# Two transfers within HBM behind each attention product: a GpSimd copy as the gate

## The chip, the cores and the metric

The kernel runs on one core of one Trainium2 chip. The metric is device time in microseconds from the first to the last instruction of the core, with what lies around them. Three runs of the kernel before took 528.51, 530.26 and 531.51 us (median 530.26 us). About 0.5% of that, 2.65 us, is what a comparison of two such kernels can tell from no change.

## The reference, cut to what matters

One decoder layer over 512 tokens of width 1024. The input is normalized, and one large projection gives the inputs of two mixers that run side by side. Mixer A is sparse attention with 8 heads in 2 groups of 4 (a compressed, a selected and a sliding branch), mixer B is retention with 4 heads in chunks of 128 tokens. Each is gated, projected and merged through a sigmoid gate per channel.

```python
h = rms_norm(x, norm_pre)
proj = h @ w_in
(q_n, k_c, v_c, k_s, v_s, k_w, v_w, g_n, z_n,
 q_r, k_r, v_r, z_r, m_a, m_b) = jnp.split(proj, split_points(), axis=-1)
...
y_a = (o_a * jax.nn.silu(z_n)) @ w_nsa_o
...
y_b = (o_b * jax.nn.silu(z_r)) @ w_ret_o
merged = jax.nn.sigmoid(m_a) * y_a + jax.nn.sigmoid(m_b) * y_b
x = x + rms_norm(merged @ w_out, norm_post)
```

The product `o_a * silu(z_n)` is formed here in eight pieces, one for each tile of 128 tokens and each group of heads. Two halves of the projections that give `m_a` and `m_b` (the blocks MA1 and MB1) are computed with seven products of sub-blocks in place of eight; for that, sums and differences of blocks of `w_in` are needed.

## The kernel before, in words

All large operands are float32, split into a high part (float32r) and a low part; a product is three matmuls (high by high, low by high, high by low). Weights come in as a stream of 512 KB tiles `raw` (four buffers) that SyncE's queue loads from HBM (line 354). A tile is cast in two halves to `whi` (mostly by ScalarE, line 197), VectorE subtracts to get `wlo` (line 209, called by `sub_split`), and a buffer comes free for the next load when both `wlo` are made.

**The order of instructions** is worked out while the kernel is built. A class `Order` holds coroutines with priorities (`od.spawn`), keeps an estimated time for TensorE (`now`), for each other engine and for the transfers, and at each step lets the first coroutine go on whose awaited time has come. What a coroutine yields is a time to wait for, a time with an engine (`yield e, "pool"` waits as well until that engine is estimated to be less than 0.7 us behind), or a condition. `od.op("pool", 900.0)` adds to GpSimd's estimate. These estimates fix only the order in which instructions stand on each engine. At run time an engine starts its next instruction when the one ahead is through and its semaphores are there.

**The stages** on TensorE: projections of the attention inputs, `hidden` (compression of keys and values), then blocks of projections (Z, MA, ZR, QK, VR ...) into which the attention heads are woven (`att_head`, `att_block`), then retention (`ret`) woven into the next blocks, then the output blocks and the final product.

**The attention product.** `att_sum` runs once for each token tile t = 3, 2, 1, 0 and group g = 0, 1. When the last product of that piece is in its PSUM bank (`bank_93` for one, `bank_94` for the next), ScalarE copies one half, VectorE adds the other (`nat<-bank,nat`, 64x512) and VectorE multiplies by the gate in place (`arena_l<-nat,arena_l`, 64x512). When all eight are there, retention may read its scores.

**The sums of weights.** `weight_sums` makes, for two blocks, the sums in HBM: eight steps, at each of them one transfer for each block, 16 in all, each of 512 KB within HBM, issued by GpSimd. Steps 0 to 3 are copies (line 334), steps 4 to 7 add to what is there (line 336; steps 6 and 7 read sums made earlier). The results (`t`) are loaded by SyncE into `raw` from 383 us on, in `seven`. The planned times are `T0 + TSTEP * k` = 110, 122, ... 290 us, in the planner's own time; nothing but the order on GpSimd's queue and the earlier step on the same data holds a transfer back at run time.

**GpSimd's other work** in that stretch is the power -0.5 of the group norm of retention, `rv<-rv,nhalf` (line 209, two columns): `ret` takes mean and variance on VectorE, GpSimd makes `rv`, and VectorE's next instructions scale the retention output by it (`arena_l<-bank,mv,rv`, line 218); the gated result is transposed on TensorE (`bank<-ident,arena_l`, line 234).

Of the kernel before, what the change touches and what calls it, by code (L numbers as in the profile page):

```python
# [10 lines left out]
FT = mybir.dt.float32  # L11
# [7 lines left out]
P = 128  # L19
# [18 lines left out]
SLACK = 700.0  # L38
WAKE = 7
HOLD = 1500.0  # L40
T0, TSTEP = 110000.0, 12000.0
DVE_BIAS = 400


# [95 lines left out]
def block_kernel(ctx: ExitStack, tc, x, xT, x0s, ws, small, w2s, norm_post, rope_r, dmask, out):  # L140
    nc = tc.nc
    V, S, G, T, DMA = nc.vector, nc.scalar, nc.gpsimd, nc.tensor, nc.sync

    sp = ctx.enter_context(tc.tile_pool(name="small", bufs=1))
# [15 lines left out]
    def at(kb, n, dt=FT):  # L160
        o = int(kb * 256)
        if dt == FR:
            return arena_r[:, o:o + n]
        assert o >= 28 * 256 or o + n <= 28 * 256
        return arena_f[:, o - 28 * 256:o - 28 * 256 + n] if o >= 28 * 256 else arena_l[:, o:o + n]
# [6 lines left out]
    od = Order()  # L172
# [23 lines left out]
    def act(o, i, func=AF.Copy, r=0.0, **kw):  # L196
        S.activation(o, i, func, **kw)  # L197
        return od.op("act", act_ns(o, i, lazy(kw.get("bias"), kw.get("scale"))) + (95 if "accum_out" in kw else 0), r)
# [9 lines left out]
    def tt(o, a, b, op, r=0.0, e="dve"):  # L208
        (V if e == "dve" else G).tensor_tensor(o, a, b, op=op)  # L209
        if op == OP.pow:  # L210
            return od.op(e, 300 + 164 * size(o), r, True)
        return od.op(e, (1.042 * size(o) + 69) if e == "dve" else (2.36 * size(o) + 77), r, e == "pool" or near(o, a, b))
# [98 lines left out]


    loads, off = [], 0
    sums = []
    for pieces in stream_shape():
        if pieces == "seven":
            b11, b12, b21, b22 = (ws[off + i * P * 1024:off + (i + 1) * P * 1024].rearrange("(p n) -> p n", p=P)
# [9 lines left out]
    def weight_sums():  # L327

        for n in range(8):
            for i, block in enumerate(sums):  # L330
                yield T0 + TSTEP * (n * len(sums) + i)
                o, a = block[n]
                if n < 4:
                    G.dma_start(o, a)
                else:
                    G.dma_start(o, a, accum_op=OP.add)
                od.op("pool", 900.0)
# [574 lines left out]
    def att_out():  # L912
        for t, g in ((t, g) for t in reversed(range(NT)) for g in range(2)):
            yield lambda: (t, g) in avs
            a = avs[t, g]
            po = yield from PO.get()
            a["po"] = po
            od.spawn(att_sum(t, g, po), 1)

    def att_sum(t, g, po):  # L920
        a = avs[t, g]
        yield lambda: a["n"] == a["total"]
        yield od.need("Z0", "Z1", "Z2", "Z3")
        m, o = slice(g * 64, g * 64 + 64), slice(64 - g * 64, 128 - g * 64)
        low = yield from NAT.get()
        yield a["e"], "act"
        e = act(low[m], po[o], r=a["e"])
        yield e, "dve"
        e = tt(low[m], po[m], low[m], OP.add, e)
        PO.put(po, e)  # L930
        yield e, "pool"
        gv = szn[m, :, t * P:(t + 1) * P]
        e = tt(gv, low[m].rearrange("p (j c) -> p j c", j=4), gv, OP.mult, e)
        NAT.put(low, e)
        od.flags.add(f"att{t}{g}")
        if all(n in od.flags for n in ATT):
            DMA.dma_start(dm, dmask.rearrange("h p c -> p h c"))
            dmr.append(od.dma(P * 2048, a["e"]))
            for o in (32, 36):
                VR[0].put((at(o, 512, FR), at(o + 2, 512, FR)))  # L940
            for _ in range(2):
                b = yield from PO.get()
                PS.put(b)
# [530 lines left out]
    od.spawn(splitter(), lambda: rank(nxt[0])())  # L1474
    od.spawn(edges(), 1)
    od.spawn(weight_sums(), 1)
    od.spawn(main(), MAIN)
    od.run()
# [28 lines left out]
def stream_shape():  # L1507

    yield [512, 512]
    yield from [[1024]] * 3  # L1510
    yield from [[560]] * 4
    yield from [[1024]] * (4 + 8)
    for b in PLAN:
        yield from ["seven"] if b in SEVEN else [[1024]] * (2 if b[0] == "NO" else 4)
    yield from [[1024]] * 8
# [67 lines left out]
```

## Time and profile before

| what | value |
|---|---|
| three runs | 528.51, 530.26, 531.51 us; median 530.26 us |
| the profiled execution | 528.24 us, span 526.5 us |
| TensorE | busy 514.9 us, 98% of the span |
| VectorE, ScalarE | 405.6 us, 290.5 us |
| GpSimd | 23.8 us |
| granted TensorE clock | 0.997 over the span |
| transfers issued by GpSimd | 16, of 512 KB each |

How to read it. Times in the views are counted from the start of the span. A timeline row gives start, duration, engine, line, operation, output and inputs, and how many instructions are merged; in brackets stands the idle time of the engine before it and what ended it. Matmuls are pipelined and their ends are modelled, so the step from one start to the next tells more of TensorE than the durations do. POOL is GpSimd, DVE is VectorE, ACT is ScalarE, SP is SyncE, PEld is TensorE's loading of stationary operands; a q behind the name is the engine's sequencer. The profiled execution took 528.24 us, 2.02 us under the median of the three runs.

### The profile page before, as it was taken

The numbers are of one execution on the slowest core, as the hardware profiler recorded it, in microseconds if no ns is written. First come the engines' busy times: TensorE is split into PE (matmuls) and PEld (weight loads), VectorE is DVE, ScalarE is ACT, GpSimd is POOL, SyncE is SP. The second block draws the span as 40 slices with busy tenths as digits, with TensorE's granted clock in tenths as the row PEclk, the third lists the DMA queues.
The fourth block names the chain that finished last, engine by engine and source line by source line (L and its number), as shares of the span: only waits on it lengthen the run. The fifth ranks groups of instructions, "written<-read, shape, count | busy, mean of one in ns | idle before, by whom it ended". The sixth has DMA issues, their size and how long they took to land.

```text
span 526.5 us, 7843 instructions
## 1 busy us (share of the span) xinstructions
PE 514.9 (98%) x2778; PEld 440.8 (84%) x2778; DVE 405.6 (77%) x980; ACT 290.5 (55%) x627; POOL 23.8 (5%) x48
## 2 busy tenths in 40 slices
PE   8989999999999999999999999999999999999995
PEld 7888888788888888888878888888788989988884
DVE  6698799989979889997886576786889867645533
ACT  6663798768557886784525353524557434323411
POOL 1002100000000000000111000000000000000000
PEclk9999999999999999999999999999999999999998
DMA  8956769601304004133543532141643726625032
GB/s 311 365 198 200 220 132 260 209 2 40 121 1 129 33 0 156 36 112 119 109 136 66 190 125 76 41 120 42 219 141 122 237 83 202 205 114 159 1 109 92
DMA packets 22456, 68.87 MB, mean 131 GB/s; under 512 B 2448, under 2 KB 3728, under 8 KB 22416
## 3 DMA queue, kind: packets, MB, share of 16 engines
q1 hardware_dynamic: 19968, 59.84, 33.9%
q0 software_dynamic: 2304, 8.39, 7.2%
q8 instruction: 22, 0.36, 0.3%
q10 hardware_dynamic: 144, 0.14, 0.1%
q14 instruction: 18, 0.15, 0.1%
HBM read 66.26 MB, written 10.49 MB: 146 GB/s over the span
## 4 chain that ended last, share of the span: by engine, by line
PE 81%; DVE 7%; DMA 7%; issue 2%; ACT 1%; SPq 1%; POOLq 0%; DVEq 0%; POOL 0%; ACTq 0%
PE bank L230 76%; DMA raw<-in_stream_dram 6%; PE bank L234 6%; DVE wlo L209 3%; DVE arena_r L209 1%; DMA arena_f<-in_xT_dram 1%; DVE arena_l L844 1%; DVE arena_f L209 1%; DVE arena_l L218 1%; ACT whi L197 0%; DVE nat L209 0%; ACT arena_l L197 0%; DVE whi L205 0%; SPq L477 0%; DVE arena_f L222 0%
## 5 line engine op out<-in xcount | busy, mean ns | idle before, releaser
L197 ACT ACTIVATE whi<-raw 128x512 fp32r<-128x512 f32 x159 | 95.7, 626 | 41.3 <-PE bank L230 32.2
L209 DVE TENSOR_TENSOR wlo<-raw,whi 128x512 fp32r<-128x512 f32 x172 | 111.7, 685 | 7.6 <-ACT whi L197 6.8
L230 PE MATMUL bank<-whi,hTh 128*128 128x512 f32 x256 | 99.7, 405 | 0.8 <-DVE arena_r L222 0.4
L230 PE MATMUL bank<-whi,hTl 128*128 128x512 f32 x256 | 96.2, 391 | 0.0
L230 PE MATMUL bank<-wlo,hTh 128*128 128x512 f32 x256 | 96.1, 391 | 0.0
L230 PE MATMUL bank<-arena_r 128*128 128x256 f32 (+2 forms) x328 | 70.7, 336 | 0.3 <-DVE arena_r L209 0.3
L230 PE MATMUL bank<-arena_r,whi 128*128 128x512 f32 (+1 forms) x208 | 63.8, 382 | 0.7 <-DVE sg L222 0.7
L197 ACT ACTIVATE arena_r<-bank 128x512 fp32r<-128x512 f32 (+2 forms) x80 | 45.2, 570 | 29.1 <-PE bank L234 27.7
L197 ACT ACTIVATE arena_l<-arena_l,stat 128x128 f32<-128x128 f32 (+3 forms) x104 | 55.3, 552 | 5.6 <-DVE stat L209 2.7
L209 DVE TENSOR_TENSOR arena_r<-bank,arena_r 128x512 fp32r<-128x512 f32 (+2 forms) x72 | 46.8, 656 | 13.8 <-ACT arena_r L197 13.1
L230 PEld LDWEIGHTS bank<-whi,hTl 128*128 128x128 f32 x256 | 48.0, 188 | 10.6
L230 PEld LDWEIGHTS bank<-arena_r 128*128 128x128 f32 x328 | 51.0, 189 | 6.5 <-DVE arena_r L209 0.6
L230 PEld LDWEIGHTS bank<-whi,hTh 128*128 128x128 f32 x256 | 48.0, 188 | 9.5 <-DVE arena_r L222 0.9
L230 PEld LDWEIGHTS bank<-wlo,hTh 128*128 128x128 f32 x256 | 48.3, 189 | 8.2
L230 PE MATMUL bank<-hTh,whi 128*128 128x512 f32 (+1 forms) x144 | 52.4, 364 | 0.0
L230 PE MATMUL bank<-hTh,wlo 128*128 128x512 f32 (+1 forms) x144 | 51.2, 355 | 0.0
L230 PE MATMUL bank<-hTl,whi 128*128 128x512 f32 (+1 forms) x144 | 51.1, 355 | 0.0
L230 PE MATMUL bank<-whi,arena_r 128*128 128x512 f32 (+1 forms) x176 | 48.7, 352 | 0.0
L230 PEld LDWEIGHTS bank<-arena_r,whi 128*128 128x128 f32 x208 | 38.8, 188 | 8.6 <-DVE sg L222 1.3
L230 PE MATMUL bank<-arena_r,wlo 128*128 128x512 f32 x96 | 37.4, 389 | 0.0
L230 PEld LDWEIGHTS bank<-whi,arena_r 128*128 128x128 f32 x176 | 32.1, 189 | 4.6
L230 PE MATMUL bank<-wlo,arena_r 128*128 128x512 f32 (+1 forms) x104 | 34.7, 343 | 0.3 <-DVE wlo L209 0.3
(164 smaller groups left out, 768.4 us busy)
## 6 DMA issues: line engine op xcount, KB each, us to landing
raw<-in_stream_dram SPq DMA_DIRECT2D x77, 512.0 KB, 4.3
t<-in_stream_dram POOLq DMA_DIRECT2D x12, 512.0 KB, 5.3
raw<-t SPq DMA_DIRECT2D x8, 512.0 KB, 3.7
arena_f<-in_rope_r_dram SPq DMA_DIRECT2D x8, 256.0 KB, 2.7
t<-t POOLq DMA_DIRECT2D x4, 512.0 KB, 5.4
arena_f<-in_xT_dram SPq DMA_DIRECT2D x8, 256.0 KB, 3.7
ends<-in_x_dram SPq DMA_DIRECT2D x4, 512.0 KB, 5.5
arena_l<-in_xT_dram SPq DMA_DIRECT2D x7, 256.0 KB, 5.7
```

The lines of the kernel that those rows point to most:

```text
L197: S.activation(o, i, func, **kw)
L209: (V if e == "dve" else G).tensor_tensor(o, a, b, op=op)
L218: V.tensor_scalar(o, a, s1, s2, op0=op0, op1=op1)
L230: T.matmul(ps, a, b, start=start, stop=stop)
L234: T.transpose(ps, a, idn)
L844: V.tensor_tensor_reduce(pv[:, b, :], sv[:, b, :], maskp[:, 512 - L:512], 1.0, -NEG, OP.add, OP.min, nm[:, b:b + 1])
```

## The change

The table of planned times goes. `weight_sums` now waits, in the order, until enough attention products are there: two transfers for each product (`PER = 2`), so step n of both blocks stands behind product n+1. To make GpSimd wait at run time too, `att_sum` lets GpSimd copy one column of the finished product into a small tile `mark`; GpSimd's instructions behind that copy, the two transfers among them, start when VectorE has written the product. The tile `mark` is read by nothing.

```diff
-T0, TSTEP = 110000.0, 12000.0
+PER = 2
...
-    sums = []
+    sums, atts = [], [0]
+    mark = sp.tile([P, 1], FT, name="mark")
...
         for n in range(8):
             for i, block in enumerate(sums):
-                yield T0 + TSTEP * (n * len(sums) + i)
+                while (n * len(sums) + i) >= PER * atts[0]:
+                    yield lambda: (n * len(sums) + i) < PER * atts[0]
                 o, a = block[n]
                 if n < 4:
                     G.dma_start(o, a)
...
         NAT.put(low, e)
         od.flags.add(f"att{t}{g}")
+        G.tensor_copy(mark[m], gv[:, 0, 0:1])
+        od.op("pool", 70.0, e)
+        atts[0] += 1
```

Because the planner's estimate of GpSimd changes, the order on the other engines changes too, from the first attention product (140 us of the trace before) to about 290 us. The numbers of instructions on TensorE stay (2767 as they stand in the order). Line numbers shift by 2 to 5, and the tiles `t` are numbered one higher.

GpSimd's queue around the last sums, before (`t` tiles are the sums in HBM, `rv` is retention's group norm):

```order
L336 DMA t_117<-in_stream_dram 128x1024
L336 DMA t_121<-in_stream_dram 128x1024
L209 TENSOR_TENSOR rv<-rv,nhalf 128x2
L336 DMA t_116<-t_117 128x1024
L209 TENSOR_TENSOR rv<-rv,nhalf 128x2
L336 DMA t_120<-t_121 128x1024
L209 TENSOR_TENSOR rv<-rv,nhalf 128x2
L336 DMA t_118<-t_116 128x1024
```

and now:

```order
L338 DMA t_118<-in_stream_dram 128x1024
L338 DMA t_122<-in_stream_dram 128x1024
L938 COPY mark<-arena_l 64x1
L338 DMA t_117<-t_118 128x1024
L338 DMA t_121<-t_122 128x1024
L938 COPY mark<-arena_l 64x1
L338 DMA t_119<-t_117 128x1024
L338 DMA t_123<-t_121 128x1024
L209 TENSOR_TENSOR rv<-rv,nhalf 128x2 x8
```

Each of the last four transfers stood behind an `rv` of its own; now all of them, and the two last copies, stand ahead of the first `rv`.

VectorE from the eighth attention product to the gated retention output of the first chunk, before (`mv` holds mean and variance, `bank` tiles are in PSUM):

```order
L209 TENSOR_TENSOR arena_l<-nat_110,arena_l 64x4x128
L209 TENSOR_TENSOR arena_r<-arena_f,arena_r 128x256
...
L1079 BN_AGGR mv<-st 128x2
L216 TENSOR_SCALAR rv<-mv 128x2
L222 SCALAR_TENSOR_TENSOR arena_r<-bank_88,rs_126,arena_r 128x512
L218 TENSOR_SCALAR arena_l<-bank_90,mv,rv 128x256 x2
L209 TENSOR_TENSOR arena_r<-arena_l,arena_r 128x512
L209 TENSOR_TENSOR arena_r<-arena_f,arena_r 128x256
L209 TENSOR_TENSOR arena_l<-arena_l,arena_f 128x512
```

and now:

```order
L209 TENSOR_TENSOR arena_l<-nat_110,arena_l 64x4x128
L209 TENSOR_TENSOR arena_r<-arena_f,arena_r 128x256
...
L1084 BN_AGGR mv<-st 128x2
L216 TENSOR_SCALAR rv<-mv 128x2
L218 TENSOR_SCALAR arena_l<-bank_89,mv,rv 128x256 x2
L209 TENSOR_TENSOR arena_r<-arena_l,arena_r 128x512
L209 TENSOR_TENSOR arena_r<-arena_f,arena_r 128x256
L209 TENSOR_TENSOR wlo<-raw,whi 128x512
L209 TENSOR_TENSOR arena_l<-arena_l,arena_f 128x512
```

The scaling by `rv` (L218) follows at once on the variance now, where one instruction stood between them, and one `wlo` stands ahead of the gated output (the last row).

TensorE from the last products of the seventh attention piece (`bank_93`) over those of the eighth (`bank_94`), the first retention scores and outputs to the transposes of the gated output; the rows left out are matmuls of 128x512 of the projection blocks and a few transposes. Before:

```order
L230 MATMUL bank_93<-arena_r 128x512 x2
...
L230 MATMUL bank_94<-arena_r 128x512 x4
...
L230 MATMUL bank_89<-arena_r 128x128
...
L230 MATMUL bank_90<-arena_r 128x256 x6
L230 MATMUL bank_93<-arena_r 128x256 x6
...
L234 MATMUL bank_92<-ident,arena_l 128x128 x4
```

and now:

```order
L230 MATMUL bank_93<-arena_r 128x512 x2
...
L230 MATMUL bank_94<-arena_r 128x512 x4
...
L230 MATMUL bank_90<-arena_r 128x128
...
L230 MATMUL bank_89<-arena_r 128x256 x6
L230 MATMUL bank_93<-arena_r 128x256 x6
...
L234 MATMUL bank_91<-ident,arena_l 128x128 x4
```

The pieces stand in the same sequence; the numbers of projection matmuls in the four gaps were 30, 9, 12 and 21, and are 33, 18, 15 and 24 now.

## The prediction

> **What bounds the kernel now.** First the page of the kernel before: its span, its engines, and the chain of work that ended last.
>
> ```profile
> span 526.5 us, 7843 instructions
> PE 514.9 (98%) x2778; PEld 440.8 (84%) x2778; DVE 405.6 (77%) x980; ACT 290.5 (55%) x627; POOL 23.8 (5%) x48
> PE 81%; DVE 7%; DMA 7%; issue 2%; ACT 1%; SPq 1%; POOLq 0%; DVEq 0%; POOL 0%; ACTq 0%
> ```
>
> TensorE is busy for 98% of the span. It does the same work after the change, so a gain can only come out of its 11.6 us of idle time, and a loss is whatever makes it wait anew. Then the stretches that the change touches (us, then busy time and count of PE, PEld, DVE, ACT and POOL, the granted clock, the DMA share, GB/s).
>
> ```profile
> 80.00:90.00 10.00, 9.94 (x71) 8.83 (x69) 9.24 (x20) 8.41 (x21) 0.42 (x1) 1.00 0.94 249
> 90.00:100.00 10.00, 9.56 (x48) 7.48 (x47) 9.20 (x19) 7.13 (x15) 0.00 (x0) 1.00 0.82 273
> ```
> ```profile
> 230.00:240.00 10.00, 10.00 (x51) 8.26 (x51) 10.00 (x21) 7.22 (x17) 0.00 (x0) 1.00 0.59 209
> 240.00:250.00 10.00, 10.00 (x55) 8.54 (x54) 7.11 (x16) 4.98 (x10) 0.63 (x1) 1.00 0.25 75
> sum 150.00, PE 149.56 PEld 126.15 DVE 127.04 ACT 95.74 POOL 6.56; mean PE 9.97 PEld 8.41 DVE 8.47 ACT 6.38 POOL 0.44
> ```
>
> From 80 to 100 us the DMA engines are 82 to 94% busy and TensorE idles for 0.50 us. From 140 to 290 us (the sum) TensorE idles for 0.44 us in 150. Now GpSimd's timeline, where the transfers are, and when single ones landed.
>
> ```profile
> 43.62 1.78 POOL L334 DMA_DIRECT2D t<-in_stream_dram  x3
> 48.80 0.53 POOL L334 DMA_DIRECT2D t<-in_stream_dram  x1 [3.39 <-issue]
> 59.83 0.85 POOL L336 DMA_DIRECT2D t<-in_stream_dram  x1 [3.45 <-issue]
> 65.41 0.84 POOL L336 DMA_DIRECT2D t<-in_stream_dram  x1 [4.73 <-issue]
> 73.98 0.81 POOL L336 DMA_DIRECT2D t<-in_stream_dram  x1 [7.74 <-issue]
> 79.59 0.83 POOL L336 DMA_DIRECT2D t<-in_stream_dram  x1 [4.80 <-issue]
> 249.37 0.72 POOL L209 TENSOR_TENSOR rv<-rv,nhalf 128x2 f32<-128x2 f32 x1 [168.95 <-DVE rv L216]
> 250.07 0.86 POOL L336 DMA_DIRECT2D t<-t  x1
> ```
> ```profile
> L336 POOL DMA_DIRECT2D t<-in_stream_dram x1: 850/850/850, 59.8 to 59.8; - x1
> DMA to landing us min/median/max: 5.3/5.3/5.3
> ```
> ```profile
> L336 POOL DMA_DIRECT2D t<-in_stream_dram x1: 838/838/838, 65.4 to 65.4; - x1
> DMA to landing us min/median/max: 8.3/8.3/8.3
> ```
> ```profile
> L336 POOL DMA_DIRECT2D t<-in_stream_dram x1: 807/807/807, 74.0 to 74.0; - x1
> DMA to landing us min/median/max: 5.3/5.3/5.3
> ```
>
> Two things stand here. Twelve of the 16 transfers go out from 43.6 to 79.6 us, far ahead of the planned times. And GpSimd is held between them: the adding transfer of 59.83 lands at 65.1 and the next goes at 65.41; that one lands at 73.7, the next goes at 73.98; that lands at 79.3, the next goes at 79.59. Each time 0.3 us after a landing, though the two work on different tiles: **an adding transfer waits until the one before it has landed, and GpSimd stands still meanwhile.** Of plain copies three go out at once.
>
> **The change, part by part.**
>
> *Twelve transfers leave the stretch of 43 to 88 us.* What they cost there, by the views of the tile `raw` (the stream of weights) from 60 to 100 us, and from 120 to 245 us, where no transfer of GpSimd runs:
>
> ```profile
>   DMA raw<-in_stream_dram: 3.4, 3
>   PEld bank L230: 1.1, 4
>   PE bank L230: 0.3, 1
> DMA to landing us min/median/max: 3.2/5.0/7.3
> ```
> ```profile
> DMA to landing us min/median/max: 3.2/3.5/5.0
> ```
>
> Loads take up to 7.3 us there against 5.0, ScalarE waited three times for one, 3.4 us in all, and TensorE for the halves made of them 0.3 us, its weight loads 1.1 us. Between the two views 1.4 us at most reached TensorE; some of the loads were only queued behind each other. I take -1.0 us, with bounds of -1.5 and 0.
>
> *The copies and the transfers now follow the eight attention products.* A copy of 64x1 is costed by the nearest rows:
>
> ```profile
> 1.25 0.10 POOL L255 MEMSET nhalf<- 128x4 f32 x1
> 34.02 0.29 POOL L209 TENSOR_TENSOR gate<-nat,cst 128x24 f32<-128x24 f32 x1 [10.26 <-ACT nat L197]
> ```
>
> So 0.1 to 0.3 us each; eight of them lie in the 169 us for which GpSimd waits anyway (row of 249.37), and cost nothing by themselves. What lies behind them on GpSimd is the question: the two last pairs of transfers, all adding, and then every `rv`. The path to the first `rv`, on VectorE and TensorE, and the pace of TensorE:
>
> ```profile
> 236.38 0.68 DVE L209 TENSOR_TENSOR arena_l<-nat,arena_l 64x512 f32<-64x512 f32 x1
> 249.12 0.17 DVE L216 TENSOR_SCALAR rv<-mv 128x2 f32<-128x2 f32 x1
> 251.98 0.68 DVE L209 TENSOR_TENSOR arena_l<-arena_l,arena_f 128x512 f32<-128x512 f32 x1
> ```
> ```profile
> 253.72 0.60 PE L234 MATMUL bank<-ident,arena_l 128*128 128x128 f32 x4
> ```
> ```profile
> 289.21 10.93 PE bank L230 x48
> ```
> ```profile
> L336 POOL DMA_DIRECT2D t<-t x4: 865/872/882, 250.1 to 285.6; - x4
> DMA to landing us min/median/max: 5.2/5.4/8.3
> ```
>
> The seventh product ends at 237.06 us. When is the first `rv` wanted? Before, its variance is ready at 249.29, 12.23 us later. In the new order 15 more projection matmuls stand on TensorE between the two (33+18+15 against 30+9+12), at 10.93/48 = 0.228 us each 3.4 us. So it is wanted at about 252.7.
>
> When is GpSimd free? With 0.3 us for a semaphore and the copy, the seventh pair starts at 237.35. A chain of four follows: transfer A, its landing, 0.3 us, B, landing, 0.3 us; the eighth copy is long possible (the eighth product ends near 244.7), but stands behind B; then C and D. D is issued after three landings and takes 0.87 us more. With 5.3 us a landing that is 237.35 + 3 x 5.6 + 0.87 = 255.0. If A lands as late as the worst adding transfer did, 8.3 us, it is 258.0. A runs beside loads (the DMA share of 0.59 from 230 to 240 us), B to D hardly (0.25). I take 6.5 us for A and 5.4 for the others: 256.4. **The first `rv` is 3.7 us late**, between 2.3 and 5.3.
>
> VectorE stands in order at the scaling by `rv`, with the gated output behind it. TensorE's transposes had 253.72 - 252.66 = 1.06 us to spare; three more matmuls ahead of them (24 against 21) give 0.7 us and one more `wlo` on VectorE takes 0.6, so 1.2 us hide a part. TensorE then stands for 3.7 - 1.2 = 2.5 us, with bounds of 1.1 and 4.1. Nothing else is in its queue for that time, and the pairs before are harmless: the sixth is through before the seventh product comes.
>
> [...]
>
> *The transfers beside the later loads.* From 120 to 245 us loads land after 3.5 us (median), most of them long before they are cast. Slowed like the earlier ones, up to 2.3 us (7.3 against 5.0), one load in four may come too late. TensorE idles for nothing of that now. I take +0.3 us, bounds 0 and +1.0.
>
> *The four transfers that stood behind an `rv`* are gone from 250 to 286 us. Their sums are loaded from 383 us on, before as now, so the term is 0:
>
> ```profile
> L357 SPq DMA_DIRECT2D raw<-t x8: 319/326/331, 383.2 to 424.9; - x8
> ```
>
> *The new order from 140 to 290 us.* The gain is bounded by the 0.44 us that TensorE idles there; for the loss the nearest row is the stretch of 80 to 100 us, which lost 0.50 in 20 us: in three such stretches 1.5. I take 0, bounds -0.4 and +1.5.
>
> The sum: -1.0 + 2.5 + 0.3 + 0 = +1.8 us, on the profiled execution's 528.24 us 530.0. That execution lies 2.02 us under the median of 530.26, against which the forecast stands: **532.0 us**, a shade slower, within what can be told from no change (0.5%, 2.65 us: 527.6 to 532.9).
>
> **The rivals.**
>
> *The hold at full price (slower).* If loads slow A to 8.3 us, `rv` is 5.3 us late and TensorE stands for 4.1; VectorE, 100% busy just before, has a backlog, the early gain is half and the order costs something too: -0.5 + 4.1 + 0.8 + 0.5 = +4.9, 535.2 us. It decides from a hold of 4.6 us on: then 3.4 us reach TensorE, and less 0.7 for the other terms that is over 2.65. For it speaks that two of four adding transfers from the stream took over 8 us; against it, that all four later ones took 5.2 to 5.6.
>
> *The loads were the bound (faster).* If all 3.4 us of ScalarE's waits come back on TensorE, through work queued behind the casts, and the hold is hidden: -3.4 + 0.3 = -3.1, 527.2 us. Against it stands TensorE's idle time of 0.50 us from 80 to 100.
>
> *No hold.* If A to D come through by 252.7, the sum is -1.0 + 0.3 = -0.7, 529.5 us. That needs landings of (252.7 - 237.35 - 0.87)/3 - 0.3 = 4.5 us, or that adding transfers within HBM do not wait for each other; the traced ones are all over 5.2. [...]
>
> That the transfers do not move at all can be left out: in the new order each pair stands behind a copy that waits for VectorE.
>
> **How the numbers follow.** The forecast gets 0.38, the full hold 0.32, the loads as the bound 0.16, no hold 0.14. Faster by over 0.5% is the loads' case, 0.16; slower the full hold, 0.32; within 0.5% the two others, 0.52. The likeliest case alone spans 529.5 to 533.5. The range that should hold 8 times in 10 takes in most of the rivals on both sides: 528.0 to 535.8.
>
> **What would show it.** Right: loads of `raw` from 60 to 100 us landing after 5 us at most, and ScalarE's 3.4 us gone; on GpSimd's timeline four issues 5.5 us or more apart after the seventh product, the first `rv` directly behind the last of them, and a wait of VectorE's L218 for `rv` of 2 to 5 us, with a TensorE wait of 1 to 4 us at the transposes behind. Wrong: the pairs issued without a gap, or the first `rv` waiting for VectorE as now; a TensorE idle time from 140 to 290 us that has other causes; or a gain from 60 to 100 us beyond 1.5 us.

## The result, and the profile after

The changed kernel takes **534.96 us** (median of 6 runs, 533.63 to 536.14) against 528.57 us (6 runs) for the kernel before in the same series: ratio on record 1.011, 95% interval 1.0078 to 1.0141, so it is slower by 1.1% (the medians alone give 6.4 us, 1.2%). The forecast was 532.0 us, within 0.5% of no change as the likeliest case. What came is nearer to the rival on the other side, "the hold at full price", for which 535.2 us was worked out.

The profiled execution took 535.38 us. Its page: span, engines, granted clock in 40 slices, and the chain of work that ended last.

```profile
span 533.6 us, 7862 instructions
PE 516.9 (97%) x2778; PEld 441.8 (83%) x2778; DVE 402.1 (75%) x974; ACT 294.6 (55%) x637; POOL 28.1 (5%) x56
PEclk9999999999999999999799999999999999999998
PE 76%; DVE 9%; DMA 6%; issue 6%; ACT 1%; POOL 1%; SPq 0%; POOLq 0%; DVEq 0%; ACTq 0%
```

TensorE's idle time went from 11.6 us to 533.6 - 516.9 = 16.7 us, its share of the chain from 81 to 76%, and one slice of the granted clock, near 260 us, shows a 7. GpSimd's timeline at that place (start, duration, engine, line, operation, output and inputs, count; in brackets the idle time before it and what ended it):

```profile
237.69 2.39 POOL L938 COPY mark<-arena_l 64x1 f32<-64x1 f32 x1 [10.14 <-DVE arena_l L209]
240.03 0.82 POOL L338 DMA_DIRECT2D t<-t  x1
247.78 0.83 POOL L338 DMA_DIRECT2D t<-t  x1 [6.94 <-issue]
248.66 0.29 POOL L938 COPY mark<-arena_l 64x1 f32<-64x1 f32 x1
253.39 0.82 POOL L338 DMA_DIRECT2D t<-t  x1 [4.44 <-issue]
259.65 0.82 POOL L338 DMA_DIRECT2D t<-t  x1 [5.44 <-issue]
260.54 0.73 POOL L209 TENSOR_TENSOR rv<-rv,nhalf 128x2 f32<-128x2 f32 x1
```

These are the forecast's copy, transfers A, B, C, D (the copy of 248.66 is the eighth) and the first `rv`, in the forecast's order, with gaps of 4.4 to 6.9 us between the issues. Only the times are later. What waited for `rv`, on VectorE's and TensorE's timelines (the last row of TensorE before its stop starts at 257.56):

```profile
252.49 0.17 DVE L216 TENSOR_SCALAR rv<-mv 128x2 f32<-128x2 f32 x1
261.30 1.00 DVE L218 TENSOR_SCALAR arena_l<-bank,mv,rv 128x256 f32<-128x256 f32 x2 [8.64 <-POOL rv L209]
```
```profile
257.56 0.39 PE L230 MATMUL bank<-whi,hTl 128*128 128x512 f32 x1
264.49 1.12 PE L234 MATMUL bank<-ident,arena_l 128*128 128x128 f32 x4 [6.55 <-DVE arena_l L209]
```

The variance is there at 252.66 us, GpSimd takes it up at 260.54: 7.9 us late. VectorE waits 8.64 us for it, where the forecast's sign was 2 to 5, and TensorE stands still for 6.55 us, where it was 1 to 4. And TensorE does not start again at full pace. The same stretch by windows (us; busy time and count of PE, PEld, DVE, ACT, POOL; granted clock, DMA share, GB/s):

```profile
257.50:260.00 2.50, 0.44 (x2) 0.02 (x1) 0.00 (x0) 1.06 (x2) 0.35 (x1) 1.00 0.16 30
260.00:262.50 2.50, 0.00 (x0) 0.00 (x0) 1.20 (x3) 0.00 (x0) 1.20 (x2) 0.73 0.59 77
262.50:265.00 2.50, 0.51 (x3) 0.51 (x4) 2.50 (x5) 0.00 (x0) 0.00 (x0) 0.50 0.81 151
265.00:267.50 2.50, 2.50 (x8) 2.06 (x7) 2.47 (x6) 1.48 (x3) 0.00 (x0) 0.50 0.53 195
267.50:270.00 2.50, 2.50 (x11) 2.00 (x10) 1.73 (x4) 1.81 (x4) 0.00 (x0) 0.91 0.64 210
```

The granted clock falls to 0.50 during the stop and is still 0.50 from 265.0 to 267.5, where TensorE is "100% busy" with 8 matmuls. Last, the early loads, by the view of the tile `raw` from 60 to 100 us:

```profile
  DMA raw<-in_stream_dram: 1.6, 2
  PEld bank L230: 0.8, 3
DMA to landing us min/median/max: 3.1/3.7/4.9
```

The landings are relieved as forecast, 4.9 us at most against 7.3. ScalarE's waits for them fell from 3.4 us to 1.6, where the forecast had them gone.

### The profile page after: what moved, and what is told of

It reads as the page before. It is cut to its first block, busy times and chain, and to the rows that moved or that the text cites. A ratio compares the mean times of both kernels' runs of the same rounds, so it can differ in the third digit from the quotient of the medians.

```text
span 533.6 us, 7862 instructions
## 1 busy us (share of the span) xinstructions
PE 516.9 (97%) x2778; PEld 441.8 (83%) x2778; DVE 402.1 (75%) x974; ACT 294.6 (55%) x637; POOL 28.1 (5%) x56
## 4 chain that ended last, share of the span: by engine, by line
PE 76%; DVE 9%; DMA 6%; issue 6%; ACT 1%; POOL 1%; SPq 0%; POOLq 0%; DVEq 0%; ACTq 0%
PE bank L230 70%; PE bank L234 5%; DMA raw<-in_stream_dram 4%; DVE wlo L209 3%; DVE arena_r L209 2%; DMA arena_l<-in_xT_dram 1%; DVE arena_l L218 1%; DVE arena_l L846 1%; DMA arena_f<-in_xT_dram 1%; DVE nat L209 1%; DVE nat L222 1%; DVE arena_f L209 1%; POOL t L338 0%; ACT arena_l L197 0%; ACT arena_f L197 0%
## 5 line engine op out<-in xcount | busy, mean ns | idle before, releaser
L197 ACT ACTIVATE whi<-raw 128x512 fp32r<-128x512 f32 x162 | 97.8, 627 | 39.9 <-PE bank L230 32.6
L197 ACT ACTIVATE arena_l<-arena_l,stat 128x384 f32<-128x384 f32 (+3 forms) x111 | 58.6, 549 | 8.1 <-DVE stat L226 4.0
L209 DVE TENSOR_TENSOR arena_r<-bank,arena_r 128x512 fp32r<-128x512 f32 (+2 forms) x72 | 46.9, 656 | 13.2 <-ACT arena_r L197 12.7
L234 PE MATMUL bank<-ident,arena_l 128*128 128x128 f32 (+1 forms) x232 | 34.4, 276 | 7.5 <-DVE arena_l L209 6.5
L234 PEld LDWEIGHTS bank<-ident,arena_l 128*128 128x128 f32 (+1 forms) x232 | 28.2, 140 | 14.3 <-DVE arena_l L209 7.0
## 6 DMA issues: line engine op xcount, KB each, us to landing
arena_f<-in_rope_r_dram SPq DMA_DIRECT2D x8, 256.0 KB, 2.6
arena_f<-in_xT_dram SPq DMA_DIRECT2D x8, 256.0 KB, 3.7
arena_l<-in_xT_dram SPq DMA_DIRECT2D x7, 256.0 KB, 5.5
```

The source lines that it names most:

```text
L234: T.transpose(ps, a, idn)
```

## The experiments

Two theories at first. **Theory 1, the hold**: all of the loss is the first `rv` standing on GpSimd behind four adding transfers. **Theory 2**: the new order of instructions, or the transfers that now run beside later loads, cost the time, and the stop only shows where. Medians (of 10 to 12 runs; of 4 for the hold alone and for the filled stop), with the ratio to the kernel before on the same chip in the same series. Its medians there were 528.42 to 528.69 us, and 528.57 beside the changed kernel, so medians of different series are compared below as they stand. Ratios and intervals are those on record, which are not quotients of the medians:

| kernel | us | ratio, 95% interval |
|---|---|---|
| the change, last four back behind `rv` | 527.24 | 0.997 (0.9958 to 0.9983) |
| the new order alone | 527.39 | 0.9976 (0.9957 to 0.9996) |
| order before, twelve transfers late | 529.80 | 1.0018 (0.9998 to 1.0037) |
| order before, the hold alone | 538.61 | 1.0187 (1.0165 to 1.0208) |
| the change, plain transfers | 526.84 | 0.9964 (0.9948 to 0.998) |
| the change, `dynamic_dma_scratch_size` 896 | 527.45 | 0.9977 (0.9959 to 0.9995) |
| the change, stop filled with matmuls | 534.07 | 1.0089 (1.0057 to 1.0121) |
| the change, three transfers a product | 526.72 | 0.996 (0.9939 to 0.9982) |
| the change, PSUM reads behind product 7 | 531.12 | 1.0062 (1.0031 to 1.0092) |

### The hold undone in the changed kernel

```diff
...
-                if n < 4:
-                    G.dma_start(o, a)
-                else:
-                    G.dma_start(o, a, accum_op=OP.add)
+                fn = lambda o=o, a=a, n=n: G.dma_start(o, a) if n < 4 else G.dma_start(o, a, accum_op=OP.add)
+                if n >= 6:
+                    late.append(fn)
+                else:
+                    fn()
...
         e = tt(rv, rv, nhalf[:, 2:4], OP.pow, e, "pool")
+        if late:
+            late.pop(0)()
```

> The changed kernel, with the same order on TensorE, VectorE, ScalarE and SyncE and all eight copies, but the last four transfers (steps 6 and 7) no longer behind the copies of products 7 and 8: each goes behind an `rv` of its own, as before the change. Only GpSimd's queue differs. Theory 1, the hold (the first `rv` stands behind four transfers): VectorE's wait for `rv` and TensorE's stop of 6.7 us at the transposes are gone, so is the low granted clock behind it; the time is the kernel before's less 0.5 us, give or take 1 (about 528 us). Theory 2, that the new order of instructions or the transfers beside later loads cost the time: nothing comes back, 533 us or more. Both theories leave the early loads relieved.

527.24 us, 7.7 us under the changed kernel, though no instruction of TensorE, VectorE, ScalarE or SyncE has another place. GpSimd's and VectorE's timelines:

```profile
237.07 2.38 POOL L939 COPY mark<-arena_l 64x1 f32<-64x1 f32 x1 [10.18 <-DVE arena_l L209]
252.17 0.73 POOL L209 TENSOR_TENSOR rv<-rv,nhalf 128x2 f32<-128x2 f32 x1 [7.67 <-DVE rv L216]
252.93 0.99 DVE L218 TENSOR_SCALAR arena_l<-bank,mv,rv 128x256 f32<-128x256 f32 x2 [0.92 <-POOL rv L209]
```

GpSimd waits for the variance now, no longer the other way round, and TensorE shows no wait for the gated output. Theory 1 stands for the whole loss. The copy lasts 2.38 us here too, with no transfer of GpSimd's issued within 10 us of it (226.06 the one before, 252.87 the one behind), so its length comes neither from the hold nor from one of those beside it.

### The new order alone

```diff
-                od.op("pool", 900.0)
+            for o, a in [block[n] for block in sums]:
+                fn = lambda ...
+                (late.append if n >= 6 else early.append)(fn)
...
-        G.tensor_copy(mark[m], gv[:, 0, 0:1])
+        while early:
+            early.pop(0)()
```

Without a copy to wait for, the twelve `early` transfers start far ahead of the products, as in the kernel before; the `late` ones follow an `rv` each.

> The changed kernel's order on TensorE, VectorE, ScalarE and SyncE without the copies and without the change's places for the transfers: the first twelve go out early, as before the change, the last four each behind an `rv`. So the new order alone. Theory 1, the hold: the order costs 0 to 1 us, 528.5 to 529.5 us. Theory 2, the order: about 534 us.

527.39 us, under the 528.5 to 529.5 expected: the new order costs nothing, it seems to gain 1.3 us (0.2 to 2.3 by the interval). Of that the trace shows 0.4: from 245 to 280 us TensorE is busy for 35.00 of 35 us, and for 34.56 in the kernel before, where it waits for one `arena_r` of line 222 that stood late in VectorE's queue. The rest is not found. Beside it the kernel above (527.24 us) is the same order with the early loads relieved: 0.15 us between them.

### The early relief alone, in the order before

```diff
+            for o, a in [block[n] for block in sums]:
+                todo.append(lambda ...)
+        late.extend(todo[12:])
+        del todo[12:]
...
+        if todo:
+            G.tensor_copy(mark[m], gv[:, 0, 0:1])
+            for _ in range(2):
+                todo.pop(0)()
...
+        if late:
+            late.pop(0)()
```

> The kernel before, in its own order, with the first twelve transfers two by two behind copies of the attention products 1 to 6, and the last four each behind an `rv` as before. So the relief of the early loads, and the load on later ones, alone. Theory 1: the kernel before's time less 0.7 us (0.5 us come back from 60 to 100 us), about 528 us. Theory 3, that transfers beside the loads of 140 to 245 us slow the weights: 2 us more than before. The rival of the prediction that early loads were the bound: 3 us less.

529.80 us, +1.1 with an interval of -0.1 to +2.0 us. The gain of 0.7 us lies outside the interval, so that expectation missed; the loss of 2 us lies on its edge and is not shown; the rival's gain of 3 us is excluded. Its twelve runs lie between 526.72 and 531.71 us.

### The hold alone, in the order before

```diff
...
         od.flags.add("gate")
+        while len(todo) > 4:
+            todo.pop(0)()
...
         od.flags.add(f"att{t}{g}")
+        if t == 0:
+            G.tensor_copy(mark[m], gv[:, 0, 0:1])
+            for _ in range(2):
+                todo.pop(0)()
```

> The kernel before, in its own order, with the first twelve transfers early, and the last four behind copies of products 7 and 8, ahead of every `rv`. So the hold alone, with no relief of the early loads. Theory 1: `rv` is wanted at 249.3 us here, 3.4 us sooner than in the changed kernel, and comes at about 257 to 260.5, so 7.7 to 11 us late; 1 us of it is hidden, and the granted clock falls behind the stop as in the changed kernel: 7 to 11 us more than before, 535.5 to 539.5 us. Theory 2 (the hold is hidden, other parts cost): within 1 us of before.

538.61 us, 9.95 us over the kernel before, inside the 7 to 11 expected. GpSimd's timeline, VectorE's row of the variance, and TensorE's row behind its stop:

```profile
235.98 2.46 POOL L938 COPY mark<-arena_l 64x1 f32<-64x1 f32 x1 [157.71 <-DVE arena_l L209]
259.12 0.73 POOL L209 TENSOR_TENSOR rv<-rv,nhalf 128x2 f32<-128x2 f32 x1
```
```profile
247.97 0.17 DVE L216 TENSOR_SCALAR rv<-mv 128x2 f32<-128x2 f32 x1
```
```profile
262.47 1.11 PE L234 MATMUL bank<-ident,arena_l 128*128 128x128 f32 x4 [9.73 <-DVE arena_l L209]
```

The variance is there at 248.14 us, `rv` is taken up at 259.12: 11.0 us late, a stop of 9.7. In the changed kernel 7.9 us late gave 6.55. Both hide 1.3 us, near the 1.2 that the forecast had taken (the kernel with PSUM reads below, 3.1 us late with a stop of 1.8, makes it 1.3 again). So the hold alone, in either order, makes the kernel slower, and the stop is the lateness less 1.3 us.

### Why the transfers hold GpSimd: plain transfers

The forecast read "an adding transfer waits until the one before it has landed" out of the trace. Is it the adding?

```diff
-                    G.dma_start(o, a, accum_op=OP.add)
+                    G.dma_start(o, a)
```

> The changed kernel with plain copies in place of the adding transfers of steps 4 to 7, same places on every queue, same bytes written (the additions are left out, so the sums of weights hold something else). If it is the adding that keeps a second transfer, and GpSimd with it, back until the first has landed: the last four go out without a gap of 4 to 7 us, in under 1 us each behind their copies, the first `rv` is made within 0.5 us of its variance, TensorE does not stop, and the time falls from the changed kernel's 535 us to 527 to 528 us. If GpSimd is held by something else (the order of the data between the steps, the copies): the gaps, the stop of 6.7 us and 535 us stay.

```profile
239.16 1.02 POOL L338 DMA_DIRECT2D t<-t  x2
252.84 0.73 POOL L209 TENSOR_TENSOR rv<-rv,nhalf 128x2 f32<-128x2 f32 x1 [5.14 <-DVE rv L216]
```

The pair goes out at once, 0.51 us an issue against 0.82 for an adding one, `rv` waits for its variance alone, and the time is 526.84 us. C and D still go one behind the other (245.89 and 247.19 us), and the trace names the data of A and B as what they wait for.

### Why the transfers hold GpSimd: 512 or 896 bytes

```diff
-    nc = bacc.Bacc("TRN2", target_bir_lowering=False, num_devices=1, dynamic_dma_scratch_size=512)
+    nc = bacc.Bacc("TRN2", target_bir_lowering=False, num_devices=1, dynamic_dma_scratch_size=896)
```

> The changed kernel with 896 in place of 512 bytes for the descriptors of GpSimd's transfers, nothing else. If an adding transfer needs more than half of that space, so that the next finds room only when the one ahead is through: two or more are in flight now, B goes out within 1 us of A, the first `rv` is at most 2 us late, TensorE stops for under 1 us, 527 to 530 us. If adding transfers are held back for another reason (one at a time by the engine's own rule): the issues stay 5 to 7 us apart and the time stays at 535 us.

```profile
240.42 1.67 POOL L338 DMA_DIRECT2D t<-t  x2
247.91 0.82 POOL L338 DMA_DIRECT2D t<-t  x1 [2.40 <-DMA t<-t]
250.40 0.81 POOL L338 DMA_DIRECT2D t<-t  x1 [1.66 <-DMA t<-t]
253.55 0.73 POOL L209 TENSOR_TENSOR rv<-rv,nhalf 128x2 f32<-128x2 f32 x1 [2.35 <-DVE rv L216]
```

527.45 us: one number undoes the loss with every transfer still adding and still ahead of `rv`. A and B go out together; C and D now wait for the data that A and B write, which is named as their releaser, where the changed kernel's rows say "issue". The last is issued by 251.2 us, before the variance is there (253.03). So the rule in the forecast was wrong as a rule. Adding transfers are not bound to go one by one: **with 512 bytes B was issued 7.75 us after A, 0.3 us after A had landed; with 896 both are issued within 1.67 us.** Issues and time came as expected; by what the number keeps B back, no trace shows.

### The granted clock behind the stop

```diff
+        if hp == 0 and t == 0:
+            for _ in range(28):
+                T.matmul(pt, hTh[:, 0, 0:P], hTh[:, 0, :], start=True, stop=True)
         for a in range(4):
```

> The changed kernel with 28 more matmuls of 128x512 (0.23 us each, 6.4 us together) on TensorE right ahead of the first transposes of the gated output; their result is overwritten. They fill the stop of 6.7 us and move nothing else. If the low granted clock from 260 to 267.5 us (0.73, 0.50, 0.50) comes from the stop: the clock stays at 1.00 there, the transposes come no later, and the time falls by 1 to 2 us against the changed kernel, though it does more work: 533 to 534 us. If the clock falls for another reason: 535 us or more and the same low clock.

TensorE's timeline and the windows of this kernel:

```profile
258.03 6.51 PE L1101 MATMUL bank<-hTh 128*128 128x512 f32 x28
264.90 0.66 PE L234 MATMUL bank<-ident,arena_l 128*128 128x128 f32 x4 [0.36 <-DVE arena_l L209]
```
```profile
262.50:265.00 2.50, 2.14 (x10) 1.44 (x10) 2.50 (x6) 0.00 (x0) 0.00 (x0) 1.00 0.90 175
265.00:267.50 2.50, 2.50 (x14) 2.12 (x15) 2.47 (x6) 1.77 (x4) 0.00 (x0) 1.00 0.65 210
267.50:270.00 2.50, 2.50 (x17) 2.27 (x16) 2.14 (x5) 1.39 (x3) 0.00 (x0) 1.00 0.60 170
```

The clock stays at 1.00, and from 265 to 270 us 31 matmuls go through where the changed kernel has 19. The transposes came 0.41 us later than there (264.90 against 264.49), as `rv` did, and the kernel still ends 0.9 us sooner (534.07 us), with 28 matmuls more. So the low clock comes from the stop and costs 0.9 + 0.4 = 1.3 us. The runs of the two kernels (533.19 to 534.23 and 533.63 to 536.14) overlap, so the 0.9 is rough; the clock is not. The two traces give the cost more directly, by the row of TensorE that stands behind the transposes and 15 matmuls in both, first of the changed kernel, then of this one (the counts depend on where the view ends):

```profile
270.07 2.19 PE L230 MATMUL bank<-arena_r 128*128 128x256 f32 x17
```
```profile
268.83 2.32 PE L230 MATMUL bank<-arena_r 128*128 128x256 f32 x18
```

The same work takes 270.07 - 264.49 = 5.58 us there and 268.83 - 264.90 = 3.93 here, so the slow restart costs 1.65 us by the traces, 1.3 by the medians.

The windows of the changed kernel's trace, cut finer, show when the clock changes: 1.00 until 261.1 us, 0.73 from 261.1 to 261.2, 0.50 from 261.2 to 267.9, 0.64 from 267.9 to 268.0 and 1.00 behind. It fell 3.2 us after the last matmul had ended (257.95), and came back 3.5 us after TensorE had started again (264.49). With the hold alone it is 0.50 from 260 to 265 us behind a stop of 9.73 us; the mean of 0.80 from 250 to 260 gives an estimated fall at 256.0, if the clock is 1.00 and then 0.50, 3.3 us after the last matmul (252.74). Behind the stop of 1.77 us in the kernel with PSUM reads below it does not drop.

### Three transfers a product

```diff
-PER = 2
+PER = 3
```

> The changed kernel with three transfers behind each attention product in place of two, so that all 16 are issued by the sixth product (about 219 us) and none stands between products 7 and 8 and the first `rv`; the two last copies stay. The planner's order shifts a little. By the theory of the hold: `rv` is made within 0.5 us of its variance, no stop of TensorE at the transposes, 527 to 528.5 us, the same as with the last four put back behind the `rv`. By the rival that transfers beside the loads of 140 to 245 us cost time: there are more of them now beside those loads, 530 us or more.

```profile
227.22 0.82 POOL L338 DMA_DIRECT2D t<-t  x1 [4.42 <-issue]
253.18 0.73 POOL L209 TENSOR_TENSOR rv<-rv,nhalf 128x2 f32<-128x2 f32 x1 [6.02 <-DVE rv L216]
```

The last transfer is issued at 227.22 us, later than the 219 expected but 25 us before the variance, and 526.72 us is the lowest median of all (plain transfers are 0.1 us from it). It beats the kernel before by 0.4% (0.2 to 0.6) and the changed kernel by 8.2 us. The cost that the rival saw in more transfers beside the loads does not show.

### The copy of 2.4 us

Seven of the changed kernel's eight copies take 0.18 to 0.51 us, the one behind product 7 takes 2.39. VectorE's timeline of the changed kernel behind that product, which ends at 237.56:

```profile
237.48 1.89 DVE L209 TENSOR_TENSOR wlo<-raw,whi 128x512 fp32r<-128x512 f32 x3
239.29 0.75 DVE L209 TENSOR_TENSOR nat<-nat,nat 128x256 f32<-128x256 f32 x2
239.96 1.28 DVE L209 TENSOR_TENSOR arena_r<-bank,arena_r 128x512 fp32r<-128x512 f32 x2
```

Five instructions in a row take both operands from SBUF; the sixth reads a PSUM bank, and the copy ends 0.12 us after its start (240.08). It is the same with the other long copies: 0.11 us behind the first PSUM-reading instruction with the last four put back, 0.13 with the hold alone, and 0.12 for a copy of 0.51 us in the changed kernel and one of 1.11 us in the kernel with the early relief alone, which had one and two such instructions ahead. One copy does not fit. In the kernel with three transfers, GpSimd's copy behind product 7 and VectorE's instructions beside it are

```profile
235.41 1.12 POOL L938 COPY mark<-arena_l 64x1 f32<-64x1 f32 x1 [7.37 <-DVE arena_l L209]
```
```profile
235.20 1.88 DVE L209 TENSOR_TENSOR wlo<-raw,whi 128x512 fp32r<-128x512 f32 x3
```

so the copy ended at 236.53, while the third of three such instructions was running (to 237.08), ahead of any that reads PSUM. A run of them thus held a copy for 2.4 us, but did not always hold it to its end; what let this one in is open. The test puts reads of PSUM in between:

```diff
+    gap = sp.tile([P, 96], FT, name="gap")
...
         e = tt(gv, low[m].rearrange("p (j c) -> p j c", j=4), gv, OP.mult, e)
         NAT.put(low, e)
+        if t == 0 and g == 0:
+            for i in range(3):
+                V.tensor_copy(gap[m], po[m, i * 96:i * 96 + 96])
```

> The changed kernel with three small reads of PSUM on VectorE (64x96 each, into a tile that nothing reads) right behind the seventh attention product, ahead of the three `wlo` and two `nat` that follow there. If GpSimd's copy of 2.39 us is kept waiting by VectorE's run of instructions with two operands from SBUF, and gets in with the first instruction that reads PSUM: the copy is over by about 238.1 us (0.2 to 0.5 us), transfer A goes out 1.9 us sooner (238.1 in place of 240.0), the first `rv` is 1.9 us sooner, TensorE's stop falls from 6.7 to about 5 us, and the time by about 2 us, to 533 us; the three reads delay VectorE by 0.4 us, which nothing waits for. If the copy is long for another reason: 2.4 us as in the changed kernel, and 535 us.

GpSimd's, VectorE's and TensorE's timelines, and a window of TensorE right behind its stop:

```profile
237.94 0.18 POOL L942 COPY mark<-arena_l 64x1 f32<-64x1 f32 x1 [10.14 <-DVE arena_l L209]
238.54 0.82 POOL L339 DMA_DIRECT2D t<-t  x1 [0.41 <-issue]
256.63 0.73 POOL L209 TENSOR_TENSOR rv<-rv,nhalf 128x2 f32<-128x2 f32 x1
```
```profile
237.74 0.81 DVE L940 COPY gap<-bank 64x96 f32<-64x96 f32 x3
260.58 0.66 PE L234 MATMUL bank<-ident,arena_l 128*128 128x128 f32 x4 [1.77 <-DVE arena_l L209]
```
```profile
260.00:262.50 2.50, 1.92 (x11) 1.67 (x12) 2.47 (x6) 1.09 (x3) 0.00 (x0) 1.00 0.73 218
```

The copy takes 0.18 us. Transfer A goes out 1.5 us sooner in the trace, and 1.75 sooner against product 7, which ended 0.26 us later here. `rv` is 3.9 us sooner, 2 more than expected, because A also landed sooner (A to B is 5.96 us against 7.75) and so did C (C to D is 5.46 us against 6.26). The stop is 1.77 us where about 5 was expected, the clock stays at 1.00, and the median is 531.12 us, 3.8 under the changed kernel. Its twelve runs reach from 529.34 to 536.23 us, and the trace is of one of the lowest, so the landing of A, not the copy, may well be what varies; no run here shows it.

So the copy took 2.39 us beside five VectorE instructions in a row with both operands from SBUF, and 0.18 beside three that read PSUM; in the kernel with three transfers it took 1.12 and was over before the end of three of the first kind. Why the one holds the other, no run shows.

### The kernel before once more

Here nothing is changed; the run is for a second trace.

> The kernel before once more, for a second trace. The relief of the early loads, forecast at 1.0 us, did not show where it was made alone, and the new order gained 1.3 us where at most 0.4 was forecast. If the traced waits are the same each time, the second trace shows TensorE idle for 11 to 12 us again, with 0.4 to 0.5 us of it from 245 to 280 us; if the idle time of the first 40 us (3.3 us in the first trace) differs by 1 us or more, then differences of 1 us between single traces, and the forecast of 1.0 us read out of one, say nothing.

530.63 us in this execution, 2.4 over the one that the forecast was read from. The windows from 80 to 100 us and from 245 to 280 us, and the view of `raw` from 60 to 100 us:

```profile
80.00:100.00 20.00, 18.25 (x110) 15.04 (x109) 17.06 (x36) 15.51 (x34) 0.83 (x1) 1.00 0.82 239
245.00:280.00 35.00, 34.56 (x186) 29.36 (x185) 27.14 (x62) 13.42 (x27) 5.00 (x6) 1.00 0.41 99
```
```profile
  DMA raw<-in_stream_dram: 3.7, 2
DMA to landing us min/median/max: 3.2/4.7/8.8
```

TensorE idles for 13.2 us in all, more than the 11 to 12 expected of equal waits; the first 40 us hold 3.3 us of it both times. From 80 to 100 us it idles for 1.75 us, where the first trace had 0.50: one load took 8.8 us this time. The 0.44 us from 245 to 280 us are there both times. So the early waits vary by over 1 us from one execution to the next, and the forecast's bound of 1.5 us on the gain was read from a mild one. Elsewhere too: over these two and six traces of other kernels the first 40 us, in which all kernels have the same order, hold between 1.65 and 3.34 us of idle time.

## Why the prediction was right, and where it was wrong

The mechanism that decides was named: the first `rv` behind four adding transfers, VectorE's scaling by it, the transposes. The time lies inside the range. But the likeliest case fell, because the term of the hold was mis-sized: +2.5 us in the sum, and **7.7 us** by the kernel with the hold undone (in the traces, a stop of 6.55 us and 1.65 us of slow restart).

- *How near the time came.* Part of it is luck. The forecast stands on the median of three runs, 530.26 us; over six runs it is 528.57, 1.7 us lower. The change was forecast at +1.8 us and measured at +6.4. Counted from its own base the range ends at +5.5 us, and the rival's sum is +4.9: the measured 534.96 us agrees with both only because the base was too high.
- *When `rv` is wanted.* 252.7 us forecast, 252.66 measured, but two differences cancel in it. Product 7 ended at 237.56, 0.5 us later than taken, and the variance followed 15.1 us behind it, where 12.23 + 3.4 = 15.65 was forecast: the 15 matmuls more made 2.9 us, not 3.4.
- *When GpSimd is free.* 256.4 forecast, 260.5 measured, so 4.1 us out. A was to start at 237.35 and started at 240.03: 0.5 us of that since product 7 came later, 2.2 in the copy, which the forecast put at 0.1 to 0.3 us from rows without VectorE's two-operand work beside them. A to B took 7.75 us against 6.8, B to C 5.61 against 5.7, C to D 6.26 against 5.7. The copy is the larger half, and the range for the lateness, 2.3 to 5.3 us, had no room for it.
- *What hides.* 1.2 us forecast, 1.3 measured.
- *What follows the stop.* Nothing forecast; the low granted clock costs 1.3 to 1.65 us more. The rival's price (4.1 us of stop) left it out as well; it came to nearly the right time by luck, with a smaller stop, a cost of the order that is not there, half the early gain lost and the high base.
- *The rule of one adding transfer at a time.* Right for the gaps, wrong as a cause: they come with 512 bytes and go with 896 (B 7.75 us behind A, or both issued within 1.67 us). The description of the kernel before, by which only the order on GpSimd's queue and the earlier step on the same data hold a transfer back at run time, lacks this too. The rival "no hold" needed the transfers not to wait for each other, and with 896 bytes A and B do not, and there is no hold: the first `rv` waits for its variance alone, as the row of 253.55 shows. Its other way, landings of 4.5 us, did not come: they took 7.4, 5.3 and 6.0 us.
- *The early relief.* -1.0 us forecast. The waits at the place fell (ScalarE's 3.4 us to 1.6, not to nothing), but in time 0.15 us show in the new order and none in the old one. At the place itself the traces do show it: from 80 to 100 us TensorE idles for 0.15 to 0.30 us in four traces with the early transfers moved (the changed kernel, the last four put back, the early relief alone, the PSUM reads), and for 0.5 to 1.75 in the four without. The rival that early loads were the bound falls with the times.
- *Later loads +0.3, new order 0.* With the hold out of the way the new order is 1.0 to 1.7 us faster than the kernel before (the five medians from 526.72 to 527.45 us), not slower. The bound of -0.4 us on that gain came from one trace; 0.4 us of it is seen, the rest stays open.
- *GpSimd's queue in order.* The hold of 2.5 us takes for granted that `rv` does not pass the transfers ahead of it, which no run had shown by then. In the changed kernel's trace the `rv` whose data had been there for 7.9 us started 0.07 us after D was issued, so the queue did not let it past.

## What to carry to other kernels

Before a small instruction is put behind transfers on GpSimd, look on its timeline for gaps between issues; here gaps that ended 0.3 us after a landing meant that each adding transfer waited for the one before it, and the `rv` queued behind four of them was taken up 7.9 us late. What undid it here was 896 bytes in place of 512, the transfers behind the latency-bound instruction, or the transfers well before it (25 us). And add to a stop of TensorE of several us the slow restart behind it (here 1.3 to 1.65 us behind 6.55), and to a GpSimd instruction that reads SBUF what VectorE's run of two-operand instructions beside it may cost (here 2.39 us in place of 0.18, beside five of them).

## What the hardware did that was not expected

- A GpSimd copy of 64x1 took 0.18 us in most places and 2.39 us beside five VectorE instructions with two operands from SBUF. It ended 0.11 to 0.13 us after the first one that read PSUM had started in the five cases compared above; in a sixth (1.12 us beside three) it ended 0.55 us before the three were through.
- With `dynamic_dma_scratch_size` at 512 one adding transfer of 512 KB was in flight at a time, but more than one plain one (A and B issued 0.51 us apart, landing after 6.3 and 7.1); at 896 two adding ones were. Landing then took 7.1 us for A and 9.1 for B, against 7.4 and 5.3 one by one.
- After 6.55 us without a matmul the granted clock was 0.50, and TensorE worked on at 0.50 for 3.5 us (from 264.49 until between 267.9 and 268.0, by the finer windows): its matmuls of 128x512 start 0.42 to 0.43 us apart from 265.84 to 267.97, and 0.22 to 0.24 apart behind. After 1.77 us without one the clock stayed at 1.00.
